# Gate products and the norm's spreading as split fp32r matmuls in place of fp32 ones

## The chip, the cores and the metric

The kernel runs on one core of a Trainium2 chip. The metric is the time of one execution on the device in microseconds (us), the median of a few runs. A core has five engines with a queue each: TensorE (PE in the profile, with its weight loads as PEld), VectorE (DVE), ScalarE (ACT), GpSimd (POOL) and SyncE (SP). Each engine works through its queue in order and waits on semaphores for the others. DMA transfers are issued from the queues of SP and POOL.

## The reference

One layer of a hybrid decoder, for 2048 tokens of width 1024, in float32:

```
h = rms_norm(x, g1)
z = h @ w_in                              # 1024 x 2560: q, k, v, xr, gr, 512 columns each
attn = dilated_attention(q, k, v)         # 8 heads, three dilations, weighted by their denominators
xr = causal_depthwise_conv(xr, conv_w, conv_b)             # 4 taps
r = sigmoid(xr @ w_r + b_r); i = sigmoid(xr @ w_i + b_i)   # in 8 blocks of 64x64
log_a = -8 r softplus(-lam); a = exp(log_a)
u = sqrt(-expm1(2 log_a)) * (i * xr)
rec_t = a_t * rec_(t-1) + u_t             # the recurrence over time
m = concat(attn, rec * gelu(gr)) @ w_out
x = x + rms_norm(m, g2)
h = rms_norm(x, g3)
x = x + rms_norm((relu(h @ w_ff_in) ** 2) @ w_ff_out, g4)
```

## The kernel before

*Products.* An input that a large product needs in more than fp32r's precision is split in two fp32r parts: `split` (lines 54 to 57) casts it into an upper part on ScalarE (line 56) and subtracts this from it for the lower part on VectorE or GpSimd (line 57). A product is then three fp32r matmuls into one bank: upper by upper, upper by lower, lower by upper. `product` does this for the input projection, eight times three matmuls of 128x512 (lines 208 to 210). Two kinds of product in the first part of the kernel are plain fp32 matmuls of unsplit operands: those of the gates and those that spread the norm.

*Stages.* Time is cut in two halves of 1024 tokens, each in two blocks (`b`, or `tb` from 0 to 3) of 512. Until about 600 us the projection of all columns, the recurrence and the attention of the first half are done; then come the output projection and the MLP of the first half, the attention of the second half, and its output projection and MLP. The order of the first part is written out in `ORDER`, `BETWEEN` and `LATER` at the end of the file: "q01" is the q, k and v products of half 0 and head pair 1, "r12" the recurrence of half 1 and channel group 2, "a0" an attention pair, "x2" the loading of block 2. Ahead of this list the groups 0 and 1 of half 0 are done at the start, with weights, x and the norms' inputs loaded from memory at once, into a pool `px` of their own that is given back afterwards.

*The start.* `load_start` loads x of block 0 and the weights of columns 12 and 16 (group 0's xr and gr) in four pieces; their four raw halves lie in tiles "wraw". Weights 13 and 17 (group 1) come through `load_w` with two halves each in the same ring of tiles, of which there are six. All these loads go through `load_next`, which makes each of them be issued on SP's queue behind the one before. `load_norm` (line 137) reads x by rows ("xn") and sums its squares on ScalarE (line 151).

*The norm's spreading.* `spread_norm` turns the factor of each of 512 tokens (tile `r_x`, 128x4) into a 128x512 tile `bc` that has it in every partition: four times a diagonal matrix (`dg`, line 196, VectorE) is multiplied by ones (line 197, TensorE, one fp32 product of 128x128), and the bank is copied out by ScalarE (line 199). It is called four times: for blocks 0 and 1 at the start, for 2 and 3 by "x2" and within "q10".

*A block of the recurrence.* `recurrent_block` runs 16 times (four groups, two halves, two blocks each). The projected xr is scaled out of its bank (line 316, VectorE), the convolution makes `xc` (its first tap on GpSimd, line 319, three on VectorE, line 322), and the two gate products, `pr` (line 325) and `pi` (line 327), multiply `xc` by a 128x128 block-diagonal weight `bd`. ScalarE takes the tanh of both (lines 330 and 332) and then th and the decay r of the sigmoid's output (lines 335 and 336); VectorE makes a2 (line 338), the factor of the input (lines 339, 341, 342) and runs the scan over time (line 343). The gelu of the other columns goes from VectorE (line 347) over GpSimd (lines 350 to 352) back to VectorE (lines 354, 355). The tiles `lt` (th), `la` (a2), `lr` and `li` have one buffer in each pool.

*The order on each engine.* No queue's order stands in the source. `Plan` traces all instructions and lets `Machine` play them through with costs for each kind: each engine takes, of the instructions whose inputs are ready and whose tile is free, the one that is needed first, and TensorE the one that comes first in the program. The resulting order on every engine is then fixed. A change of a few instructions is so planned anew with all others. Each engine takes its instructions in the planned order on the chip, and where a planned input comes later than planned, it waits with all that stand behind.

*Other tiles that the change names.* In the attention of a first half, `fold` (line 420) brings the upper 64 partitions of a bank down, and `join` makes the weights of the two branches in a tile `jt` (lines 691 to 703) that is stored by line 705. `zh` and `zl` hold the parts of q and k on the way to memory, `t512` the scaled products.

Of the kernel before, what the change touches and what calls it, by code (L numbers as in the profile page):

```python
# [9 lines left out]
F32 = mybir.dt.float32  # L10
# [6 lines left out]
P = 128  # L17
# [22 lines left out]
def f32(ap):  # L40
    return ap.bitcast(F32)
# [47 lines left out]
class Project:  # L89
# [14 lines left out]
    def load_w(self, hf, ct, lo_eng=None, px=None):  # L104
# [5 lines left out]
        for half in range(2):  # L110
            k0 = half * (KT // 2)
            raw = (px or self.pa).tile([P, KT // 2, P], F32, tag="wraw", bufs=6 if px else 2, name=f"wraw{hf}_{ct}_{half}")
            self.load_next(raw, self.w_in[ct, :, k0:k0 + KT // 2, :], px)
            split(nc, hi[:, k0:k0 + KT // 2, :], lo[:, k0:k0 + KT // 2, :], raw, lo_eng=lo_eng or self.lo)
        return hi, lo

    def load_start(self, cts, px):
# [4 lines left out]
        raws = {ct: [p.tile([P, KT // 2, P], F32, tag="wraw", bufs=6, name=f"wraw0_{ct}_{i}") for i in range(2)] for ct in cts}  # L122
# [67 lines left out]
    def spread_norm(self, tb):  # L190
# [3 lines left out]
        for j in range(TB // P):  # L194
            dg = self.pa.tile([P, P], F32, tag="dg", bufs=2, name=f"dg{tb}_{j}")
            nc.vector.tensor_scalar(out=dg, in0=self.cst["ident"], scalar1=r[:, j:j + 1], scalar2=None, op0=ALU.mult)
            nc.tensor.matmul(pbc[:, j * P:(j + 1) * P], self.cst["ones"], dg, start=True, stop=True)
# [61 lines left out]
    def recurrent_consts(self, conv_w, conv_b, w_r, b_r, w_i, b_i, lam):  # L259
# [9 lines left out]
        for nm, a in (("r", w_r), ("i", w_i)):  # L269
            t = self.bd[nm] = p.tile([P, 4, P], F32, tag=f"bd_{nm}", name=f"bd_{nm}")  # L270
            g.memset(t, 0.0)
            for u in range(2):
                nc.gpsimd.dma_start(out=t[u * HD:(u + 1) * HD, :, u * HD:(u + 1) * HD], in_=a[u])

# [33 lines left out]
    def recurrent_block(self, hf, c, b, wx, wg, px, zx=None):  # L308
# [15 lines left out]
        pr = self.bank("X", f"pr{n}")  # L324
        pe.matmul(pr, self.bd["r"][:, c, :], xc, start=True, stop=True)
        pi = self.bank("O" if px else "X", f"pi{n}")
        pe.matmul(pi, self.bd["i"][:, c, :], xc, start=True, stop=True)
# [52 lines left out]
def attention(tc, p, bank, cst, scr, hf, mask_a_d, mask_b_d, pj, pw=None, px=None, first=None):  # L380
# [36 lines left out]
    def fold(dst, o, pat, **kw):  # L417

        t = p.tile([HD, TB], F32, tag="fold", bufs=1, name="fold")
# [250 lines left out]
    def join(pr, st, na, nb):  # L670
# [18 lines left out]
        jt = pj.tile([P, TB], F32, tag="jt", bufs=1, name=f"jt{hf}_{pr}")  # L689
# [66 lines left out]
SMB = (3, 4)  # L756
WB = 5
# [1192 lines left out]
def trunk(tc, x, xT, g1, g2, g3, g4, w_in, conv_w, conv_b, w_r, b_r, w_i, b_i, lam, w_out, w1, w2,  # L1950
# [11 lines left out]
    with (  # L1962
# [8 lines left out]
        cst["ones"] = c.tile([P, P], F32, name="ones")  # L1971
        nc.vector.memset(cst["ones"], 1.0)
# [39 lines left out]
        with contextlib.ExitStack() as st:  # L2012
            p1a = st.enter_context(sb("p1a", "left"))
            p1 = st.enter_context(sb("p1", "left"))
# [219 lines left out]
```

## Time and profile before

| | |
|---|---|
| runs | 2175.87 us median of 3 (2174.74 to 2176.11) |
| the profiled execution | 2174.38 us, of which the span of instructions is 2172.6 us |
| TensorE busy | 2136.3 us, 10264 matmul passes |
| VectorE, ScalarE, GpSimd busy | 1520.6, 1229.1, 482.5 us |
| TensorE's clock granted | 0.999 of full speed |
| DMA | 473.51 MB, 218 GB/s in the mean |

Rows of the profile give engine, source line, operation, and output and inputs by their tiles' names, with the number of instructions and their duration. In rows by time the first number is the start in us from the start of the span, the second the length; in brackets stands how long the engine was idle before, and what ended that. Matmuls overlap each other by their latency: the rate is read from the distance of their starts or ends, not from their durations. An fp32 matmul shows as two passes. Rows of windows give the stretch, its length, the busy time of TensorE, its weight loads, VectorE, ScalarE and GpSimd with the number of instructions, then TensorE's clock, the DMA engines' share and the rate in GB/s; where they are asked for one source line, only the engines that this line uses are listed.

### The profile page before, as it was taken

The numbers are of one execution on the slowest core, as the hardware profiler recorded it, in microseconds if no ns is written. First come the engines' busy times: TensorE is split into PE (matmuls) and PEld (weight loads), VectorE is DVE, ScalarE is ACT, GpSimd is POOL, SyncE is SP. The second block draws the span as 40 slices with busy tenths as digits, with TensorE's granted clock in tenths as the row PEclk, the third lists the DMA queues.
The fourth block names the chain that finished last, engine by engine and source line by source line (L and its number), as shares of the span: only waits on it lengthen the run. The fifth ranks groups of instructions, "written<-read, shape, count | busy, mean of one in ns | idle before, by whom it ended". The sixth has DMA issues, their size and how long they took to land.

```text
span 2172.6 us, 30852 instructions
## 1 busy us (share of the span) xinstructions
PE 2136.3 (98%) x10264; PEld 1754.5 (81%) x10264; DVE 1520.6 (70%) x2893; ACT 1229.1 (57%) x2486; POOL 482.5 (22%) x556
## 2 busy tenths in 40 slices
PE   8999999999999999999999999999999999999998
PEld 6777888777788788888888888878788888888887
DVE  7858667858878777775776868787766565664456
ACT  7537566634554655554766667764455555654442
POOL 4652534567523001000010101113100000000003
PEclk9999999999999999999999999999999999999999
DMA  7557686358765667779777785796634444866665
GB/s 249 174 157 212 199 259 194 120 185 296 222 229 180 247 255 296 280 271 356 240 227 222 231 259 170 229 297 192 230 129 174 146 153 146 327 203 193 193 192 183
DMA packets 224548, 473.51 MB, mean 218 GB/s; under 512 B 23476, under 2 KB 79572, under 8 KB 218116
## 3 DMA queue, kind: packets, MB, share of 16 engines
q1 hardware_dynamic: 195572, 337.52, 48.7%
q0 software_dynamic: 28816, 134.01, 17.3%
q8 instruction: 81, 1.33, 0.3%
q14 instruction: 79, 0.65, 0.1%
HBM read 337.09 MB, written 151.13 MB: 225 GB/s over the span
## 4 chain that ended last, share of the span: by engine, by line
PE 84%; DVE 6%; ACT 5%; issue 2%; POOL 2%; DMA 1%; DVEq 0%; POOLq 0%; ACTq 0%; SPq 0%
PE o L1234 9%; PE o L1236 9%; PE o L1235 9%; PE za L1085 5%; PE za L1086 5%; PE za L1084 5%; PE z L210 4%; PE z L209 4%; PE z L208 4%; PE m L871 3%; PE m L870 3%; PE m L869 3%; PE zc L1084 3%; PE zc L1085 3%; PE zc L1086 3%; PE oB L652 2%
## 5 line engine op out<-in xcount | busy, mean ns | idle before, releaser
L208 PE MATMUL z<-hH,wH 128*128 128x512 f32 x640 | 254.6, 399 | 7.3 <-ACT wH L56 5.1
L209 PE MATMUL z<-hL,wH 128*128 128x512 f32 x640 | 256.8, 402 | 0.4 <-DVE hL L183 0.4
L210 PE MATMUL z<-hH,wL 128*128 128x512 f32 x640 | 254.3, 399 | 0.0
L208 PEld LDWEIGHTS z<-hH,wH 128*128 128x128 f32 x640 | 120.7, 189 | 35.0 <-ACT wH L56 5.6
L209 PEld LDWEIGHTS z<-hL,wH 128*128 128x128 f32 x640 | 120.8, 189 | 28.5 <-issue 3.8
L210 PEld LDWEIGHTS z<-hH,wL 128*128 128x128 f32 x640 | 120.8, 189 | 25.7 <-issue 3.6
L57 POOL TENSOR_TENSOR wL<-wraw,wH 128x512 fp32r<-128x512 f32 x70 | 96.0, 1384 | 55.9 <-ACT wH L56 54.4
L1089 ACT ACTIVATE sq<-sq 128x512 f32<-128x512 f32 x93 | 58.8, 632 | 76.6 <-DVE sq L1093 76.6
L1149 POOL DMA_DIRECT2D sa<-sq x31 | 16.5, 532 | 376.6 <-ACT sq L1090 363.7
L432 ACT ACTIVATE smB<-smB,stB 128x128 f32<-128x128 f32 (+3 forms) x128 | 71.5, 560 | 41.5 <-DVE stB L426 41.2
L432 ACT ACTIVATE sm<-sm,stA 128x256 f32<-128x256 f32 (+1 forms) x128 | 63.4, 497 | 53.6 <-DVE stA L426 53.4
L57 DVE TENSOR_TENSOR tlB<-pT_B,thB 128x384 fp32r<-128x384 f32 x96 | 57.1, 598 | 30.4 <-ACT thB L56 27.6
L1090 ACT ACTIVATE sq<-sq 128x512 f32<-128x512 f32 x124 | 76.9, 630 | 2.6
L56 ACT CAST wH<-wraw 128x512 fp32r<-128x512 f32 (+1 forms) x84 | 47.8, 596 | 43.9 <-PE z L209 28.0
L1268 POOL TENSOR_TENSOR y<-y,g4b 128x512 f32<-128x512 f32 x8 | 12.4, 1573 | 257.1 <-ACT junk_y L86 257.1
L426 DVE CUSTOM_DVE_ANT_0 smB<-SB,mask_b 128x128 f32<-128x128 f32 (+3 forms) x128 | 59.3, 485 | 7.3 <-PE SB L627 5.8
L426 DVE CUSTOM_DVE_ANT_0 sm<-S,mask_a 128x256 f32<-128x256 f32 (+1 forms) x128 | 47.5, 408 | 23.4 <-PE S L569 23.3
L405 PE MATMUL pT_B<-ident,smB 128*128 128x128 f32 x320 | 59.9, 277 | 1.7 <-DVE tlB L57 0.9
L240 DVE TENSOR_TENSOR zn<-z,bc 128x512 f32<-128x512 f32 x32 | 22.0, 688 | 54.4 <-PE z L210 52.0
L56 ACT CAST thB<-pT_B 128x384 fp32r<-128x384 f32 x96 | 48.9, 511 | 18.9 <-PE pT_B L405 15.1
L322 DVE SCALAR_TENSOR_TENSOR xc<-xr,cw,xc 128x512 f32<-128x512 f32 x48 | 52.9, 1110 | 6.0 <-POOL xc L319 5.6
L57 POOL TENSOR_TENSOR zl<-zn,zh 128x512 fp32r<-128x512 f32 x28 | 39.4, 1408 | 61.9 <-ACT zh L56 52.5
(607 smaller groups left out, 7075.9 us busy)
## 6 DMA issues: line engine op xcount, KB each, us to landing
sa<-as POOLq DMA_DIRECT2D x31, 1024.0 KB, 6.8
w1r<-in_dram SPq DMA_DIRECT2D x56, 512.0 KB, 4.3
sa<-sq POOLq DMA_DIRECT2D x31, 768.0 KB, 4.0
wraw<-in_dram SPq DMA_DIRECT2D x76, 256.0 KB, 3.5
place<-in_dram SPq DMA_DIRECT2D x14, 1024.0 KB, 6.7
sb<-place POOLq DMA_DIRECT2D x14, 1024.0 KB, 4.2
kh<-sk SPq DMA_DIRECT2D x24, 512.0 KB, 5.1
kl<-sk SPq DMA_DIRECT2D x24, 512.0 KB, 6.8
```

Source lines behind the costliest of these rows:

```text
L57: (lo_eng or nc.vector).tensor_tensor(out=lo, in0=src, in1=f32(hi), op=ALU.subtract))
L208: pe.matmul(z, hi[:, k, :], hh, start=(k == 0), stop=False)
L209: pe.matmul(z, hi[:, k, :], hl, start=False, stop=False)
L210: pe.matmul(z, lo[:, k, :], hh, start=False, stop=(k == KT - 1))
L426: v.tensor_tensor_reduce(out=sm[:, c0:c0 + w], in0=sp[:, c0:c0 + w], in1=mask[:, mask.shape[-1] - w:], scale=1.0, scalar=3.0e38, op0=ALU.a ...
L432: s.activation(out=sm[:, c0:c0 + w], in_=sm[:, c0:c0 + w], func=AF.Exp, scale=-1.0, bias=st[:, 0, u, cols[j]:cols[j] + 1], accum_out=st[:, ...
L1084: pe.matmul(o, hi[:, k], bh[:, k], start=start and k == 0, stop=False, skip_group_check=True)
L1085: pe.matmul(o, hi[:, k], bl[:, k], start=False, stop=False, skip_group_check=True)
L1086: pe.matmul(o, lo[:, k], bh[:, k], start=False, stop=k == KH - 1, skip_group_check=True)
L1234: pe.matmul(o, ah[:, ts], bh, start=fresh and j == 0, stop=False, skip_group_check=True)
L1235: pe.matmul(o, ah[:, ts], bl, start=False, stop=False, skip_group_check=True)
L1236: pe.matmul(o, al[:, ts], bh, start=False, stop=j == NJ - 1, skip_group_check=True)
```

## The change

The gates' products and the norm's spreading become split fp32r products. `xc` is split in parts `xh` and `xl`, in the tiles that th and a2 take later in the same block. The gates' weights are split once, from raw tiles in the ring "t512", into two fp32r tiles each. A gate is then three matmuls of 128x512 into one bank. In the spreading, the factor is split, each part makes four diagonals in one VectorE instruction (in the tiles `zh` and `zl`), and one matmul of 128x512 with ones in fp32r takes each part. To make room, the raw weights of the start have four buffers in place of six, and `jt` of the first half shares the buffer of `fold`, which is taken in full height.

```diff
-            raw = (px or self.pa).tile([P, KT // 2, P], F32, tag="wraw", bufs=6 if px else 2, ...)
+            raw = (px or self.pa).tile([P, KT // 2, P], F32, tag="wraw", bufs=RAWS if px else 2, ...)
...
-        raws = {ct: [p.tile([P, KT // 2, P], F32, tag="wraw", bufs=6, ...
+        raws = {ct: [p.tile([P, KT // 2, P], F32, tag="wraw", bufs=RAWS, ...
...
         pbc = self.bank("X", f"pbc{tb}")
-        for j in range(TB // P):
-            dg = self.pa.tile([P, P], F32, tag="dg", bufs=2, name=f"dg{tb}_{j}")
-            nc.vector.tensor_scalar(out=dg, in0=self.cst["ident"], scalar1=r[:, j:j + 1], scalar2=None, op0=ALU.mult)
-            nc.tensor.matmul(pbc[:, j * P:(j + 1) * P], self.cst["ones"], dg, start=True, stop=True)
+        n = TB // P
+        parts = [p.tile([P, n], F32R, tag=f"rs_{x}", bufs=2, name=f"r{x}{tb}") for x in "hl"]
+        split(nc, *parts, r)
+        for x, part in enumerate(parts):
+            dg = self.pa.tile([P, n, P], F32R, tag=("zh", "zl")[x], bufs=1, name=f"dg{tb}_{x}")
+            nc.vector.tensor_tensor(out=dg, in0=self.cst["ident"].unsqueeze(1).to_broadcast([P, n, P]),
+                                    in1=f32(part).unsqueeze(2).to_broadcast([P, n, P]), op=ALU.mult)
+            nc.tensor.matmul(pbc, self.cst["ones"], dg.rearrange("p n c -> p (n c)"), start=(x == 0), stop=(x == 1))
...
-            t = self.bd[nm] = p.tile([P, 4, P], F32, tag=f"bd_{nm}", name=f"bd_{nm}")
+            t = self.pa.tile([P, 4, P], F32, tag="t512", bufs=3, name=f"bd_{nm}")
+            self.bd[nm] = [p.tile([P, 4, P], F32R, tag=f"bd_{nm}{x}", name=f"bd_{nm}{x}") for x in "HL"]
             g.memset(t, 0.0)
...
+            split(nc, *self.bd[nm], t)
...
-        pr = self.bank("X", f"pr{n}")
-        pe.matmul(pr, self.bd["r"][:, c, :], xc, start=True, stop=True)
-        pi = self.bank("O" if px else "X", f"pi{n}")
-        pe.matmul(pi, self.bd["i"][:, c, :], xc, start=True, stop=True)
+        xh = p.tile([P, TB], F32R, tag="lt", bufs=1, name=f"xh{n}")
+        xl = p.tile([P, TB], F32R, tag="la", bufs=1, name=f"xl{n}")
+        split(nc, xh, xl, xc, lo_eng=GATE_LO and g)
+
+        def gate(tag, nm):
+            z = self.bank(tag, f"p{nm}{n}")
+            hi, lo = [t[:, c, :] for t in self.bd[nm]]
+            pe.matmul(z, hi, xh, start=True, stop=False)
+            pe.matmul(z, hi, xl, start=False, stop=False)
+            pe.matmul(z, lo, xh, start=False, stop=True)
+            return z
+
+        pr = gate("X", "r")
+        pi = gate("O" if px else "X", "i")
...
-        t = p.tile([HD, TB], F32, tag="fold", bufs=1, name="fold")
+        t = p.tile([P, TB], F32, tag="fold", bufs=1, name="fold")[0:HD]
...
-        jt = pj.tile([P, TB], F32, tag="jt", bufs=1, name=f"jt{hf}_{pr}")
+        jt = pj.tile([P, TB], F32, tag="jt" if hf else "fold", bufs=1, name=f"jt{hf}_{pr}")
...
+GATE_LO = None
+RAWS = 4
...
-        cst["ones"] = c.tile([P, P], F32, name="ones")
-        nc.vector.memset(cst["ones"], 1.0)
+        cst["ones"] = c.tile([P, P], F32R, name="ones")
...
+            one = p1a.tile([P, P], F32, tag="zh", bufs=1, name="one")
+            nc.vector.memset(one, 1.0)
+            nc.scalar.copy(out=cst["ones"], in_=one)
```

With `GATE_LO` none, the lower part of `xc` is made on VectorE.

More of the change, by code (lines that the diff above doesn't have):

```diff
@@ L111, in load_w @@
             k0 = half * (KT // 2)
-            raw = (px or self.pa).tile([P, KT // 2, P], F32, tag="wraw", bufs=6 if px else 2, name=f"wraw{hf}_{ct}_{half}")
+            raw = (px or self.pa).tile([P, KT // 2, P], F32, tag="wraw", bufs=RAWS if px else 2, name=f"wraw{hf}_{ct}_{half}")
             self.load_next(raw, self.w_in[ct, :, k0:k0 + KT // 2, :], px)
@@ L121, in load_start @@
             made[ct] = [p.tile([P, KT, P], F32R, tag=f"w{x}", bufs=4, name=f"w{x}0_{ct}") for x in "HL"]
-        raws = {ct: [p.tile([P, KT // 2, P], F32, tag="wraw", bufs=6, name=f"wraw0_{ct}_{i}") for i in range(2)] for ct in cts}
+        raws = {ct: [p.tile([P, KT // 2, P], F32, tag="wraw", bufs=RAWS, name=f"wraw0_{ct}_{i}") for i in range(2)] for ct in cts}
         jobs = list(START)
```

## The prediction

> **What bounds the kernel now.** I read the head of the page first, then the chain, then the windows by stage, then TensorE's own waits, and last the rows of the lines that the diff touches.
>
> ```profile
> span 2172.6 us, 30852 instructions
> PE 2136.3 (98%) x10264; PEld 1754.5 (81%) x10264; DVE 1520.6 (70%) x2893; ACT 1229.1 (57%) x2486; POOL 482.5 (22%) x556
> PEclk9999999999999999999999999999999999999999
> PE 84%; DVE 6%; ACT 5%; issue 2%; POOL 2%; DMA 1%; DVEq 0%; POOLq 0%; ACTq 0%; SPq 0%
> ```
>
> TensorE is busy for 98% of the span at the full clock, and 84% of the chain that ended last lies on it. So work taken off TensorE counts almost one for one, unless the stage in which it lay is one where TensorE waits for something else. Both kinds of stage are there (windows: length, then busy time of each engine):
>
> ```profile
> 0.00:80.00 80.00, 70.88 (x286) 53.06 (x287) 62.36 (x122) 62.95 (x105) 37.83 (x51) 1.00 0.65 222
> 80.00:520.00 440.00, 433.34 (x2289) 353.01 (x2288) 301.92 (x639) 236.62 (x551) 221.47 (x210) 1.00 0.64 197
> 520.00:580.00 60.00, 55.00 (x220) 40.34 (x219) 57.03 (x63) 33.53 (x48) 46.77 (x55) 1.00 0.77 255
> 580.00:2172.00 1592.00, 1577.07 (x7475) 1308.12 (x7473) 1099.29 (x2069) 896.04 (x1785) 176.43 (x243) 1.00 0.67 222
> ```
>
> From 80 to 520 us TensorE is idle for 6.7 of 440 us: its bound. In the first 80 us it is idle for 9.1 us, 5.1 of them before the first weights, and VectorE carries 62.4. From 520 to 580 us VectorE is busy for 57.0 of 60 us and TensorE idle for 5.0: there the recurrence on VectorE sets the pace. TensorE's own waits say the same; the lines of this change are among the first of them (total, times, longest):
>
> ```profile
> PE z L208 <- ACT wH L56: 5.1, 1, 5.1
> PE pr L325 <- DVE xc L322: 4.3, 5, 1.2
> PE pbc L197 <- DVE dg L196: 2.2, 3, 1.3
> PE z L208 <- DVE gr L347: 2.0, 2, 1.7
> ```
>
> **The change, part by part: what TensorE saves.** The chain shows an fp32 gate product as two passes of one product, and the fp32r products after it one by one; the second fence shows how many gate passes there are, and where.
>
> ```profile
> 71.74 0.86 PE pi L327 x2
> ...
> 72.83 0.23 PE z L210
> ...
> 79.90 0.23 PE z L208
> ```
>
> ```profile
> L325 PE MATMUL pr<-xc,bd_r x32: 590/592/697, 38.9 to 573.1; 128*128 128x512 f32 x32
> ...
> 0.00:80.00 80.00, 4.18 (x8) 1.43 (x8) 1.00 0.65 222
> 80.00:520.00 440.00, 8.37 (x16) 2.68 (x16) 1.00 0.64 197
> 520.00:580.00 60.00, 4.47 (x8) 1.19 (x8) 1.00 0.77 255
> ```
>
> An fp32 product takes 0.86 us. From 72.83 to 79.90 there are 31 fp32r steps of the same 128x512 size, so one is 7.07/31 = 0.228 us, and three are 0.68. The 32 passes of L325 are 16 products, those of L327 as many: 32 products, each cheaper by 0.86 - 0.68 = 0.18 us, or **5.7 us**. By stage: 8 products (1.4 us) before 80 us, 16 (2.9) from 80 to 520, 8 (1.4) from 520 to 580. [...]
>
> The norm's spreading, between two fp32r products:
>
> ```profile
> 30.49 0.40 PE L209 MATMUL z<-hL,wH 128*128 128x512 f32 x1
> 30.72 0.61 PE L197 MATMUL pbc<-dg,ones 128*128 128x128 f32 x4
> 31.09 0.47 PE L210 MATMUL z<-hH,wL 128*128 128x512 f32 x1
> 31.40 0.39 PE L208 MATMUL z<-hH,wH 128*128 128x512 f32 x1
> ...
> L197 PE MATMUL pbc<-dg,ones x32: 270/275/377, 28.8 to 328.3; 128*128 128x128 f32 x32
> L196 DVE TENSOR_SCALAR dg<-ident,r_x x16: 272/280/1310, 27.5 to 323.4; 128x128 f32<-128x128 f32 x16
> ```
>
> From 30.49 to 31.40 lie two fp32r steps and four passes of L197: 0.91 - 0.46 = 0.45 us for four, 0.91 for the eight of one spreading. Two fp32r products of 512 columns take 0.46. Four spreadings save 4 x 0.45 = **1.8 us**, half of it at the start. TensorE has 7.5 us less to do in all, 2.3 of them in the first 80 us, 3.8 between 80 and 520, 1.4 between 520 and 580.
>
> **What the other engines get.** Prices from the nearest rows of the same size, and the rows on which the waits rest:
>
> ```profile
> 522.12 0.69 DVE L57 TENSOR_TENSOR e_5L<-e_5L,e_5H 128x512 fp32r<-128x512 f32 x1
> 531.33 3.97 DVE L339 SCALAR_TENSOR_TENSOR th<-a,th 128x512 f32<-128x512 f32 x1
> ...
> 553.78 0.69 DVE L342 TENSOR_TENSOR i<-i,th 128x512 f32<-128x512 f32 x1
> 554.58 1.28 DVE L343 TENSOR_TENSOR_SCAN xc<-r,state,i 128x512 f32<-128x512 f32 x1
> ...
> 23.79 0.60 ACT L56 CAST wH<-wraw 128x512 fp32r<-128x512 f32 x1
> ...
> 555.96 0.69 ACT L330 ACTIVATE r<-pr,vec_br 128x512 f32<-128x512 f32 x1 [0.43 <-DVE xc L343]
> ...
> 572.61 1.12 PE L325 MATMUL pr<-xc,bd_r 128*128 128x512 f32 x2 [1.19 <-DVE xc L322]
> ```
>
> *The split of xc.* Each of the 16 blocks gets an upper part on ScalarE (0.60 us) and a lower part on VectorE (0.69 us), one behind the other, between the last tap of the convolution and the gates. Every block's gates come 1.3 us later, and VectorE has 11 us more in all, ScalarE 10. A gate that still finds its place in TensorE's queue costs nothing; where TensorE already stands at the gate (L325 above, 4.3 us in five waits, 1.19 of it at 572.61) it stands longer. Bounds for one block: 0 and 0.69 + 0.60 + 3.3, the last being what the two-input row at 531.33 took over the 0.69 of an undisturbed one.
>
> From 80 to 520 us I take 0 for the eight blocks: the cover is the products of q, k and v, of 24 steps each, which need nothing from the recurrence. Without that cover it would be 8 x 1.3 = 10 us. From 520 to 580 us the four subtractions are 2.8 us on an engine that is busy 57 of 60; since splits of early factors lie in the same stretch and can give way, I take **2.2 us**. At the start the four blocks come while VectorE is dense, but products of the first queries follow as filler: half of 2.8, **1.4 us**.
>
> *Shared tiles.* The upper part takes th's buffer and the lower part a2's, one each. So the next block's cast waits for L342 of the block before. At 553.78 L342 ends at 554.47; cast, subtraction behind the scan (to 556.5) and the last gate products would put the first tanh near 557.2, where it is at 555.96 now: 1.2 us, the same delay as above and not a second one, as the tanh had to wait for the scan (L343) anyway.
>
> *Raw weights, four buffers for six.* The rows of the start (issue on SP's queue, VectorE, ScalarE, DMA share and rate, TensorE):
>
> ```profile
> 10.95 0.98 SPq L159 DMA_DIRECT2D wraw<-in_dram  x2
> 12.94 2.48 SPq L159 DMA_DIRECT2D xn<-in_dram  x4
> ...
> 15.44 0.76 DVE L57 TENSOR_TENSOR wL<-wraw,wH 128x256 fp32r<-128x256 f32 x2
> ...
> 22.73 1.06 ACT L151 ACTIVATE xn<-xn 128x1024 f32<-128x1024 f32 x1 [0.16 <-DMA xn<-in_dram]
> ...
> 14.00:16.00 2.00, 1.62 (x7) 1.00 (x7) 2.00 (x6) 1.86 (x4) 0.00 (x0) 1.00 1.05 386
> ...
> 28.79 0.71 PE L197 MATMUL pbc<-dg,ones 128*128 128x128 f32 x4 [1.31 <-DVE dg L196]
> ```
>
> The second half of weight 13, issued near 11.4 now, takes the buffer of the second half of weight 12, which is free when the splits at 15.44 are through, near 16. SP's queue issues these loads in a fixed order, so xn, weight 17 and the second block of x all go behind it: about 4.6 us later in the queue. The DMA engines had work queued until some 15 us, so they lose about 2.3 us of a stretch in which they are full (share 1.05). The last xn then comes 2.3 us later than 22.73, and with it the norm, unless ScalarE's order hides some; weight 17 misses its product by about as much. TensorE already stands 1.31 us for that norm at 28.79, and the delay of weight 17 partly takes the place of it. Bounds 0 and 4.6; I take **1.0 us**.
>
> *Small ones.* The spreading's VectorE work goes from 4 x 0.28 to 2 x 0.69 and a small split, 0.5 us more, beside 0.45 less on TensorE before the norm is out: 0, and at most 4 x 0.5 where TensorE waits (L196 above). Its diagonals take the buffers of q's and k's parts, free at the start, and hidden by attention later. The gates' weights are cast at the start, 2 x 0.60 and 2 x 0.69, needed only at 38.9: hidden.
>
> ```profile
> L705 SPq DMA_DIRECT2D sco<-jt x8: 324/335/533, 221.8 to 425.3; - x8
> L691 DVE COPY jt<-pst x4: 269/280/281, 215.2 to 416.6; 16x128 f32<-16x128 f32 x4
> ```
>
> The joining tile now shares its buffer with the folds. It is held from 215.2 to the store at 221.8, 6.6 us, and the next pair's first fold needs it only after a pair's scores: 0, and 6.6 for each of three joins if that cover went.
>
> **Sum.** -7.5 + 1.4 + 2.2 + 1.0 = -2.9 us. The profiled execution took 2174.4 us (span 2172.6), 1.5 below the median of 2175.87; so it becomes 2171.5, and the median **2173.0**, 0.13% faster. No change can be told from one within 0.2%, 4.35 us, with this kernel.
>
> **The rivals.** *The saving comes in full*: the new latency is hidden everywhere, since all queues but TensorE's program order are planned around it and 580 to 600 us has room on VectorE. For it speaks that TensorE's waits for xc are only 4.3 us. 2175.9 - 7.5 = 2168.4.
>
> *All of it is given back*: start and end cost 7 us in place of 4.6, with small losses at the spreadings. 2176 to 2179.
>
> *Slower: VectorE and GpSimd on the shared reads.* The mechanism is the row at 531.33: an operation with two inputs in SBUF that takes 3.97 us in place of 0.69 beside GpSimd's gelu. The change adds 16 such operations, right ahead of the gates. If eight of them (from 455 us and at the start) stand 1.7 us each and TensorE with them, that is 13.6 us against 7.5, 2182; it decides from 1.5 us each. [...] Against it speaks that the undisturbed row of the same subtraction is at 0.69 in the same stretch.
>
> *The change doesn't do what it says*: fp32r products at another rate than 0.228 us. The 31 steps exclude it.
>
> **How the numbers follow.** Forecast, own range 2170 to 2176: 0.42. In full, 2168.4: 0.25. Given back: 0.15. Slower, 2182: 0.18. Faster by over 0.2% (below 2171.5) is the full saving and a third of the forecast's range, 0.39; slower (above 2180.2) 0.18; the rest 0.43. For 8 in 10 I leave out the tails of both outer cases: 2166.5, the full saving with 1.9 us of better order elsewhere (80 to 520 us has 6.7 of idle time), to 2182.
>
> **What would show it.** Right: gate products as three steps of 0.23 us; TensorE's busy time down by about 7; idle time of 520 to 580 us up by some 2; xn issued near 16 us in place of 12.94. Wrong: TensorE's wait for xl growing far past 4.3 us, or the windows after 580 us, in which nothing is edited, moving by more than 2 us.

## The result, and the profile after

The changed kernel takes **2185.72 us** (median of 5, 2181.01 to 2187.01), the kernel before 2175.85 (2174.58 to 2176.11): a ratio of 1.0044 with an interval of [1.0033, 1.0056], 9.9 us slower. The profiled execution took 2181.01 us and is the shortest of the five; the other four have a mean clock of 0.995 or 0.996 in place of its 0.997. So the trace shows 6.6 of the 9.9 us, and the rest lies in the executions with that lower clock, of which there is no trace.

The head of the page of the changed kernel, then its windows by stage (columns as in the prediction):

```profile
span 2179.2 us, 30957 instructions
PE 2138.9 (98%) x10272; PEld 1762.7 (81%) x10272; DVE 1528.1 (70%) x2907; ACT 1244.3 (57%) x2513; POOL 484.3 (22%) x556
```

```profile
0.00:80.00 80.00, 70.77 (x286) 56.19 (x287) 61.88 (x116) 59.61 (x104) 37.74 (x49) 0.98 0.66 225
80.00:520.00 440.00, 433.92 (x2285) 354.85 (x2285) 306.64 (x654) 252.82 (x573) 222.82 (x211) 1.00 0.63 193
520.00:580.00 60.00, 54.31 (x229) 42.18 (x228) 56.89 (x65) 33.22 (x49) 44.86 (x51) 1.00 0.79 264
580.00:620.00 40.00, 36.45 (x156) 28.94 (x155) 27.56 (x41) 19.53 (x32) 7.22 (x8) 0.96 0.77 255
```

TensorE was to be busy for 7 us less and is busy for 2.6 us more. In the last window it is not busy all the time any more, and its clock is below 1.00; the kernel before had this there:

```profile
580.00:620.00 40.00, 40.00 (x182) 33.04 (x181) 23.03 (x39) 20.95 (x36) 6.46 (x8) 1.00 0.83 275
```

**The gates did become three short steps.** TensorE by time, changed kernel, one gate:

```profile
523.41 0.40 PE L337 MATMUL pr<-xh,bd_rH 128*128 128x512 f32 x1
...
524.57 0.39 PE L338 MATMUL pr<-xl,bd_rH 128*128 128x512 f32 x1
524.80 0.39 PE L339 MATMUL pr<-xh,bd_rL 128*128 128x512 f32 x1
525.02 0.40 PE L213 MATMUL z<-hL,wH 128*128 128x512 f32 x1
```

Each takes some 0.23 us, and the order on TensorE has put the cover of two other products between upper and lower part, as foreseen.

**But every step of the input projection has grown.** The product just ahead of this, first in the changed kernel (15 steps), then the same stretch before (18):

```profile
519.68 0.39 PE L214 MATMUL z<-hH,wL 128*128 128x512 f32 x1
...
523.17 0.39 PE L214 MATMUL z<-hH,wL 128*128 128x512 f32 x1
```

```profile
519.71 0.39 PE L210 MATMUL z<-hH,wL 128*128 128x512 f32 x1
...
523.79 0.39 PE L210 MATMUL z<-hH,wL 128*128 128x512 f32 x1
```

3.49/15 = 0.2327 us against 4.08/18 = 0.2267 in these stretches. Over the whole projection the mean step goes from 0.2281 to 0.2313 us (steps between two of its products, without the half clock), and over its 1920 steps that is 6 us.

**And TensorE stands at the start of the output projection.** SP's queue and TensorE by time and a window, all of the changed kernel; then SP's queue before:

```profile
599.33 1.09 SPq L252 DMA_DIRECT2D sk<-zl  x2
601.64 0.38 SPq L260 DMA_DIRECT2D sv<-vs  x1
602.07 3.97 SPq L822 DMA_DIRECT2D woL<-swo  x6
```

```profile
608.07 1.65 PE L887 MATMUL m<-woH,m_0H 128*128 128x512 f32 x3 [2.68 <-ACT woH L56]
```

```profile
602.00:614.00 12.00, 8.54 (x33) 6.48 (x32) 7.92 (x14) 5.98 (x11) 0.60 (x1) 0.86 0.96 343
```

```profile
594.50 5.59 SPq L804 DMA_DIRECT2D woL<-swo  x8
```

The weights of that projection are asked for 7.6 us later. TensorE stands 2.68 us for them, and then the granted clock is at a half, 0.50 from 607.53 to 610.94 us: 0.86 in the mean of the 12 us.

**The account.** Taking the end of each matmul less the end of the one before, against the undisturbed step of its form, TensorE's time up to the first products of the output projection splits into work at undisturbed steps, what the fp32r steps are longer, standing, and what the half clock adds (us, one profiled execution each; start latency and short gaps are in "standing" of both):

| | end | work | longer steps | standing | half clock |
|---|---|---|---|---|---|
| before | 608.9 | 556.5 | 4.2 | 48.3 | 0.0 |
| changed | 615.2 | 548.9 | 10.3 | 53.6 | 2.4 |

Work falls by 7.6 us (the prediction's 7.5), and 6.1, 5.3 and 2.4 come back: 6.2 us later. Up to the last matmul of the kernel the difference is 6.6. Next to nothing more is lost in the 1560 us behind, which were not edited.

### The profile page after: what moved, and what is told of

Read it like the earlier page. It is cut to its first block, busy times and chain, and to the rows that moved or that the text cites. A ratio compares the mean times of both kernels' runs of the same rounds, so it can differ in the third digit from the quotient of the medians.

```text
span 2179.2 us, 30957 instructions
## 1 busy us (share of the span) xinstructions
PE 2138.9 (98%) x10272; PEld 1762.7 (81%) x10272; DVE 1528.1 (70%) x2907; ACT 1244.3 (57%) x2513; POOL 484.3 (22%) x556
## 4 chain that ended last, share of the span: by engine, by line
PE 84%; DVE 5%; ACT 5%; DMA 2%; issue 1%; POOL 1%; SPq 0%; DVEq 0%; ACTq 0%; POOLq 0%
PE o L1252 9%; PE o L1254 9%; PE o L1253 9%; PE za L1103 5%; PE za L1104 5%; PE za L1102 5%; PE z L213 5%; PE z L212 5%; PE z L214 5%; PE m L887 3%; PE m L888 3%; PE m L889 3%; PE zc L1103 2%; PE zc L1102 2%; PE zc L1104 2%; PE oB L668 2%
## 5 line engine op out<-in xcount | busy, mean ns | idle before, releaser
L57 POOL TENSOR_TENSOR wL<-wraw,wH 128x512 fp32r<-128x512 f32 x70 | 96.9, 1395 | 66.2 <-ACT wH L56 65.8
L57 DVE TENSOR_TENSOR tlB<-pT_B,thB 128x384 fp32r<-128x384 f32 x96 | 57.0, 598 | 33.5 <-ACT thB L56 31.1
L244 DVE TENSOR_TENSOR zn<-z,bc 128x512 f32<-128x512 f32 x32 | 22.0, 687 | 48.3 <-PE z L214 47.1
L57 POOL TENSOR_TENSOR zl<-zn,zh 128x512 fp32r<-128x512 f32 x28 | 39.2, 1399 | 69.6 <-ACT zh L56 61.3
L887 PE MATMUL m<-woH,m_0H 128*128 128x512 f32 x128 | 50.7, 404 | 2.7 <-ACT woH L56 2.7
```

What stands on the lines that cost most here:

```text
L57: (lo_eng or nc.vector).tensor_tensor(out=lo, in0=src, in1=f32(hi), op=ALU.subtract))
L887: pe.matmul(o, mh, wh[:, ds], start=(k == order[0]), stop=False)
```

## The experiments

Ratios are to the kernel before, on the same chip. "Aligned" is the changed kernel with the edit of the first experiment. The order of every queue is planned anew wherever instructions change; where the order stayed, it is said.

### Where the tiles lie

The norm's new parts `rs_h` and `rs_l` add 128 bytes per partition ahead of x's lower parts of the second block and the weights. In the kernel before, all tiles of x and of the weights begin at 448 bytes past a multiple of 512; in the changed one, x's upper parts, the first block's lower ones and the weights of the start do, while nearly all of the rest begin at 64. Three kernels with the order of all queues unchanged:

```diff
# e1_after_align, from the changed kernel
-        parts = [p.tile([P, n], F32R, tag=f"rs_{x}", bufs=2, ...
+        parts = [self.pl.tile([P, n], F32R, tag=f"rs_{x}", bufs=2, ...
# e2_before_pad, from the kernel before
-        bcast = p.tile([P, TB], F32, tag="bc", bufs=2, name=f"bc{tb}")
+        bcast = p.tile([P, TB + 16], F32, tag="bc", bufs=2, name=f"bc{tb}")[:, 0:TB]
# e3_after_shift_all, from the changed kernel
-        parts = [p.tile(...
+        parts = [self.pa.tile(...
```

> The changed kernel with one tag moved: the two parts of the norm's factor (128 bytes in a partition) lie in the recurrence's pool in place of the projection's. All instructions and their order on every engine stay the same; only the tiles behind them in the projection's pool move down by 128 bytes, so that x's second block and the weights stand to x's first block at a multiple of 512 bytes, as they did before the change. Theory A, the place in SBUF: the fp32r step of the projection, 231 ns in the changed kernel up to 600 us and 227.5 before, goes back to 227.5; 2000 steps times 3.9 ns, 7 to 8 us less, a time of 2174 to 2179 us. Theory B, the load: the steps are slower because ScalarE and VectorE carry the splits and the order is another one; then the step stays at 231 and the time at 2181 to 2187 us.

> The kernel before with each of the two norm tiles bc taken 64 bytes wider and the rest unused; instructions and orders are those of before, but x's second block and the weights move up by 128 bytes against x's first block. Theory A (place): the step rises from 227.5 to about 231 ns up to 600 us, 7 to 8 us more, 2182 to 2184 us. Theory B (load): no change, 2175 to 2176 us.

> The changed kernel with the parts of the norm's factor in the pool ahead of the projection's: all of x and the weights of after 80 us now have the same remainder by 512 bytes, but another one (64) than before (448); the weights of the start keep 448. Same instructions and orders. If what counts is how the tiles stand to each other: step 227.5 ns from 80 us on, 2175 to 2180 us. If it is the remainder itself: 231 ns, 2181 to 2187 us. Theory B (load): 231 ns, 2181 to 2187 us.

Measured: e1 **2187.46** us (1.0054 [1.0042, 1.0066]), e2 **2179.09** (1.0013 [1.0004, 1.0021]), e3 **2186.49** (1.0050 [1.0039, 1.0061]). The steps do as the placement says. TensorE by time, first the padded kernel before (22 steps), then the aligned changed one (27 steps):

```profile
523.23 0.40 PE L209 MATMUL z<-hL,wH 128*128 128x512 f32 x1
...
528.37 0.40 PE L210 MATMUL z<-hH,wL 128*128 128x512 f32 x1
```

```profile
520.27 0.39 PE L214 MATMUL z<-hH,wL 128*128 128x512 f32 x1
...
526.39 0.39 PE L214 MATMUL z<-hH,wL 128*128 128x512 f32 x1
```

5.14/22 = 0.2336 and 6.12/27 = 0.2267 us. In e3, where x and weights moved together, the mean step is 0.2278 from 80 us on, but 0.2311 before that, where the first weights lie at 448 and x at 64. So in these runs what counts is how the tiles stand to each other; 128 bytes cost 3% of a step in the stretches shown and 1.4% in the mean.

But taking the 6 us away brought nothing. In e1 TensorE arrives earlier at the same waits, stands longer, and the clock falls. Its account: work 548.9, longer steps 4.0, standing 62.1, half clock 10.5, end 625.5. This trace is of the slowest of e1's five executions (2192.41), that of the changed kernel of its fastest, so the two accounts stand further apart than the medians, which are level. This is what makes the rest of the study necessary: in this order the steps got 6 us shorter, and the end did not come earlier. The other way round work does count: in e2's trace, with the order of before, the steps are 6 us longer and the stage ends at 614.6 in place of 608.9, though by the medians the run loses only some 3 us.

### VectorE stands behind GpSimd

The largest new wait of e1 is near 303 us, in the spreading of block 2. VectorE, GpSimd and TensorE of e1 by time, and two windows:

```profile
302.77 4.11 DVE L199 TENSOR_TENSOR dg<-ident,rh 128x512 fp32r<-128x512 f32 x1
306.81 0.28 DVE L442 CUSTOM_DVE_ANT_0 sm<-S,mask_a 128x128 f32<-128x128 f32 x1
...
307.71 0.86 DVE L199 TENSOR_TENSOR dg<-ident,rl 128x512 fp32r<-128x512 f32 x1
```

```profile
302.61 1.29 POOL L57 TENSOR_TENSOR wL<-wraw,wH 128x512 fp32r<-128x512 f32 x1
303.85 1.26 POOL L746 TENSOR_TENSOR na<-na,co 128x512 f32<-128x512 f32 x1
305.07 1.26 POOL L57 TENSOR_TENSOR wL<-wraw,wH 128x512 fp32r<-128x512 f32 x1
306.54 1.48 POOL L749 TENSOR_TENSOR nb<-nb,co 128x512 f32<-128x512 f32 x1 [0.21 <-DMA co<-sco]
```

```profile
307.59 0.55 PE L585 MATMUL S<-kh,qa 128*128 128x256 f32 x1 [3.91 <-DVE stA L442]
```

```profile
303.00:307.00 4.00, 0.67 (x5) 0.40 (x4) 4.00 (x2) 0.00 (x0) 3.79 (x4) 0.83 0.67 164
307.00:313.00 6.00, 5.41 (x22) 4.66 (x23) 3.78 (x16) 4.07 (x15) 3.73 (x4) 0.55 1.05 379
```

The upper diagonals begin 0.16 us after GpSimd's subtraction, and end only when three GpSimd instructions in a row are through and GpSimd pauses (306.33). The softmax's statistics stand behind them, TensorE for these, 3.91 us; then its clock is at 0.55 for 6 us. In the changed kernel as it is, with the same order on every engine, the two operations took 1.11 and 1.73 us:

```profile
302.70 1.11 DVE L199 TENSOR_TENSOR dg<-ident,rh 128x512 fp32r<-128x512 f32 x1
```

```profile
301.95 1.30 POOL L57 TENSOR_TENSOR wL<-wraw,wH 128x512 fp32r<-128x512 f32 x1
303.20 1.74 POOL L746 TENSOR_TENSOR na<-na,co 128x512 f32<-128x512 f32 x1
304.91 1.27 POOL L57 TENSOR_TENSOR wL<-wraw,wH 128x512 fp32r<-128x512 f32 x1
```

GpSimd runs the same three here without a pause. The diagonals arrive 0.75 us after its first one began, end 0.56 us after that one has ended, and GpSimd's second takes 1.74 us in place of 1.26. In e1 they arrived 0.16 us after it and ended 0.55 us after the third. Why it ended behind the first in the one kernel and behind the third in the other isn't shown.

Does the form with one input from SBUF mend it, or a planner that doesn't put these diagonals beside GpSimd?

```diff
# e10_one_input_diagonals, aligned
-            nc.vector.tensor_tensor(out=dg, in0=ident..., in1=f32(part)..., op=ALU.mult)
+            for j in range(n):
+                nc.vector.tensor_scalar(out=dg[:, j, :], in0=self.cst["ident"], scalar1=f32(part)[:, j:j + 1], ...)
# e18_planner_knows_lock, aligned, in Machine.shared
-            big > 1 or big and isinstance(self.ins[k], mybir.InstTensorCopy))
+            big > 1 or big and isinstance(self.ins[k], (mybir.InstTensorCopy, mybir.InstTensorTensor)))
```

> The changed kernel with tiles aligned, and each part's diagonals made as four VectorE operations with one input from SBUF (a scalar per partition) in place of one operation with two. Theory A (the two-input form waits for GpSimd): no diagonal takes over 1.5 us, the 4 us wait of TensorE near 303 us and the half clock behind it are gone; VectorE has 4 x 0.9 us more; time 4 to 6 us below the aligned kernel of before (2187.5), so 2181 to 2184. Rival B (VectorE stands there for another reason, such as a queue order): the wait stays, 2186 to 2189.

> The aligned changed kernel (2187.5), with the planner told that the two-input diagonals cannot run beside GpSimd; the work is the same. If the unknown lock made the wait at 303 us: no diagonal of over 2 us, no wait of TensorE over 2 us between 300 and 310 us, and 3 to 6 us less, 2181 to 2185. If GpSimd's run of instructions there is not foreseen by the planner anyway: the wait stays in some form, and the time is 2185 to 2192.

e10: **2180.32** us (1.0023 [1.0014, 1.0031]), 7 below the aligned kernel. e18: **2181.55** (1.0026 [1.0016, 1.0036]), 6 below. Both times are near those foreseen. In e10 no diagonal takes over 1.88 us and TensorE stands at most 1.9 us for the statistics. But the form isn't what decides. In e18 the first diagonals stand nearly as long as in e1 (3.76 us for 4.11), and TensorE stands 2.0 us, for probabilities in place of statistics; in e16 (below) a small one-input diagonal stands (3.52 us, where the kernel before has 0.28 in the median); and in e14 (below), which spreads the norm in the old way, two subtractions for x do (8.64 us together). VectorE by time of e18, e16 and e14:

```profile
300.24 3.76 DVE L199 TENSOR_TENSOR dg<-ident,rh 128x512 fp32r<-128x512 f32 x1
```

```profile
305.94 3.52 DVE L196 TENSOR_SCALAR dg<-ident,r_x 128x128 f32<-128x128 f32 x1
```

```profile
299.54 8.64 DVE L183 SCALAR_TENSOR_TENSOR hL<-xr,g_sb,hH 128x512 fp32r<-128x512 f32 x2 [1.36 <-ACT hH L182]
```

So the theory that the new two-input form is the cause is too narrow. At this place one of VectorE's SBUF operations stood through a whole run of GpSimd instructions (three in e1, 4.11 us, in e9, 4.10, in e16, 3.52, and in e18, 3.76; five behind the second subtraction of e14), or behind one alone, as in the changed kernel, 1.11 us. The order decides which operation meets GpSimd there; with one and the same order it was 4.11 us in e1 and 1.11 in the changed kernel, which differ in the time of arrival, and what rule this follows isn't shown. That there is a lock, as e18's label and expectation have it, was the author's supposition: the traces show when the operations began and how long they took.

### Each part alone

```diff
# e4_gates_only, from the changed kernel: the spreading's lines as before
-        split(nc, *parts, r)
...
+            nc.vector.tensor_scalar(out=dg, in0=self.cst["ident"], scalar1=r[:, j:j + 1], ...)
# e9_spread_align, from the kernel before: the spreading's lines as changed
+        parts = [self.pl.tile([P, n], F32R, tag=f"rs_{x}", ...
+        split(nc, *parts, r)
...
# e5_before_raws4, from the kernel before (both places)
-            raw = (px or self.pa).tile([P, KT // 2, P], F32, tag="wraw", bufs=6 if px else 2, ...
+            raw = (px or self.pa).tile([P, KT // 2, P], F32, tag="wraw", bufs=4 if px else 2, ...
# e13_share_only, from the kernel before; the order of all queues stays
-        t = p.tile([HD, TB], F32, tag="fold", bufs=1, name="fold")
+        t = p.tile([P, TB], F32, tag="fold", bufs=1, name="fold")[0:HD]
-        jt = pj.tile([P, TB], F32, tag="jt", bufs=1, ...
+        jt = pj.tile([P, TB], F32, tag="jt" if hf else "fold", bufs=1, ...
```

> Only the gates are split, with the four raw buffers and the shared tiles; the norm is spread by fp32 products as before (its diagonals in the two tiles zh and zl in turn), and without the factor's parts the tiles stand as before the change. Theory A: step 227.5 ns; the gates' saving of 5.7 us less what the recurrence's end costs, 2172 to 2179 us. Theory B: 231 ns, 2179 us or more, since nearly all of the added work of ScalarE and VectorE is here. If the output projection stands for its weights near 605 us and the clock falls after it as in the changed kernel, that belongs to the gates' split and not to the spreading.

> The spreading alone as split fp32r products (gates, raw tiles, joining tile as before), with the factor's parts in the recurrence's pool so that x and the weights stand to each other as before. Theory A (the loss is made by the gates' split and by the blocked diagonal, each on its own): the third spreading near 303 us shows a two-input diagonal of about 4 us and TensorE standing 3 to 4 us behind it, the rest is as before; 1.8 us are saved on TensorE, some 4 lost, with half clock after it up to 1.7 more: 2177 to 2181. Rival B (the spreading is harmless and all of the loss is the gates'): 2172 to 2176. Rival C (any newly planned order loses): 2180 or more, with waits in places where nothing is edited.

> The kernel before with four raw tiles at the start in place of six; nothing else is edited, and the orders differ only in the first 80 us. If the ring is a cost of the change: xn issued near 16 us in place of 12.94, TensorE idle 1 to 4.6 us more in the first 100 us, 2176 to 2181 us. If the start hides it: within 1 us of the kernel before.

> The kernel before with only the joining tile sharing the buffer of the folds; the order of every queue stays as before. If the shared buffer makes the waits of TensorE for the joins near 325 us seen in the changed kernel, they appear here too and the time rises by 2 to 6 us: 2178 to 2182. If it doesn't: 2175 to 2177, no wait of over 1 us there.

Measured: gates alone **2183.97** (1.0040 [1.0027, 1.0053]); spreading alone **2189.69** (1.0066 [1.0054, 1.0079]); four raw buffers 2175.18 (0.9994 [0.9985, 1.0003]); shared joining tile 2176.89 (1.0004 [0.9995, 1.0013]). The last two cost nothing. The smaller edit costs the most: spreading alone is slower than both together. In e9 the diagonals of 303 us stand again (4.10 us, from 305.0), with further waits where nothing is edited (2.60 us for xc from 562, 2.98 for zn from 585) and five stretches of half clock before the output projection (7.1 us in its account below). Its trace, too, is of the slowest of its executions. Losses that are not additive, and do not grow with the edit, point to the order.

### The gates' work and their wait

```diff
# e7_no_xl, aligned
-        split(nc, xh, xl, xc, lo_eng=GATE_LO and g)
+        s.copy(out=xh, in_=xc)
-            pe.matmul(z, hi, xl, start=False, stop=False)
# e8_lo_pool, aligned: the lower part of xc on GpSimd
-GATE_LO = None
+GATE_LO = True
# e14_split_unused, from the kernel before: no product reads xh or xl
+        xh = p.tile([P, TB], F32R, tag="lt", bufs=1, name=f"xh{n}")
+        xl = p.tile([P, TB], F32R, tag="la", bufs=1, name=f"xl{n}")
+        split(nc, xh, xl, xc)
         pr = self.bank("X", f"pr{n}")
         pe.matmul(pr, self.bd["r"][:, c, :], xc, start=True, stop=True)
```

> The changed kernel with the tiles back in place, without the lower part of xc: each gate is upper by upper and lower by upper, which leaves out the product with xl, and VectorE's subtraction with it. 32 products (7.3 us) and 16 subtractions (11 us of VectorE) less. If VectorE and its place in the chain between convolution and gates set the first 600 us: waits for the gates fall by more than a half, and the time falls by more than the 7.3 us of the products, to 2172 to 2178 us. If TensorE's work sets it: 7 us less than 2187, 2180. If it is neither (the order, the other engines): the idle time grows by what the products save, 2185 to 2188 us.

> The changed kernel with the tiles back in place, and the lower part of xc subtracted by GpSimd in place of VectorE: 1.3 us for 0.69 in each of 16 blocks. If VectorE's load costs the time: VectorE has 11 us less, 2 to 6 us less than 2187. If the latency between convolution and gates does: 0.6 us more for each block, 2187 to 2193 us, with longer waits for the gates' second product.

> The kernel before with xc split in its two parts in all 16 blocks (in the tiles of th and a2, as in the change), but the gates stay fp32 products of the whole xc and wait for neither part; the parts are not read by any product. Theory A1 (the added work on VectorE and ScalarE, with the shared tiles, makes the loss of the gates): 2180 to 2185. Theory A2 (the gates' longer way from xc to the product makes it): 2175 to 2179.

Measured: e7 **2181.33** (1.0024 [1.0013, 1.0035]), e8 **2185.07** (1.0038 [1.0026, 1.0051]), e14 **2179.09** (1.0015 [1.0006, 1.0024]). e7 leaves out one of a gate's three terms and is 6 us below the aligned kernel, for 7.3 us less of work and 16 subtractions less; that is no more than a new order of the aligned kernel brings by itself (e12 below). Against the kernel before it has 541.6 us of work for 556.5, 14.9 less, and is still slower: standing is 62.7 for 48.3 and the half clock takes 5.6. Of those 14.9 us nothing reaches the end. Its time is nearest to the one foreseen if TensorE's work sets the pace (2180), but as a new order alone brings as much, e7 can't tell the two apart; what speaks against it is that the shorter steps of e1 and e3 brought nothing in an order that stayed. The lower part on GpSimd changes little. The unused split costs 3 us, at the upper end of what was foreseen if the gates' longer way made the loss, and under what was foreseen if the added work made it. The largest new wait in its trace is the one behind the 8.64 us above (TensorE 5.0 us for the statistics), not one at a gate.

### The loads of the output projection

```diff
# e6_wo_pool, aligned
-            nc.sync.dma_start(out=f32(lo[:, ds]), in_=w_out[k][:, ds])
+            (nc.sync if hf else nc.gpsimd).dma_start(...)
```

> The changed kernel with the tiles back in place, and the first half's output weights loaded from GpSimd's queue in place of SP's; the orders differ from the run with the tiles in place only around 600 us. Theory C: these loads stand in SP's queue behind the stores of the last k and v, come late, TensorE stands 3.3 us for woH and the clock falls after it; then both go, 4 to 7 us less than the 2187 us with the tiles in place alone, 2180 to 2183 us. Rival: the loads wait for memory that the recurrence gives back, not for the queue; then the wait for woH stays, and the time within 2 us of 2187.

**2192.93** us (1.0075 [1.0063, 1.0088]), slower still. GpSimd's queue and TensorE's waits from 600 us:

```profile
607.19 0.60 POOL L373 DMA_DIRECT2D smix<-ge  x1 [8.77 <-DVE ge L371]
607.79 3.68 POOL L822 DMA_DIRECT2D woL<-swo  x7
```

```profile
PE m L887 <- ACT woH L56: 4.8, 1, 4.8
```

Gates alone, e9, e10 and e12 have no wait for woH at all, and e12 does the same work as e1, which has 2.74 us of it: this wait, too, comes with the order. On SP's queue the loads stood behind stores of q and k; here they stand behind the last store of the recurrence, which waits 8.77 us for a VectorE operation planned behind another product. A better queue wasn't found; whether the loads could go earlier on any queue stays open.

### The order

One constant of the planner (the time from an engine's end to TensorE's start) was changed, which alters no instruction and replans every queue:

```diff
-SLACK = 0.8
+SLACK = 0.9   # e11_before_new_plan, the kernel before
+SLACK = 0.7   # e17_before_plan_07, the kernel before
+SLACK = 0.7   # e12_aligned_new_plan; e15_one_input_new_plan; e16_gates_new_plan (gates alone)
```

> The kernel before with one constant of its planner changed (the time between an engine's end and TensorE's start taken as 0.9 us in place of 0.8), so that every queue's order is planned anew while the work is the same. Theory C (before's order is a lucky one, and any new plan loses 5 to 10 us): 2180 or more. Theory A (the loss belongs to the added work): within 3 us of before, 2173 to 2179.

> The aligned changed kernel with the same constant of the planner at 0.7 in place of 0.8: the same work in another order. Theory C (the order was an unlucky one): 2180 or less is possible, as much above or below the aligned kernel's 2187.5 as the before kernel moves with its new plan. Theory A (the loss belongs to the added work): 2184 to 2191, the waits near 80, 303 and 530 us being there again.

> The aligned changed kernel with one-input diagonals and the planner's constant at 0.7 in place of 0.8. If the two gains (7 us by the diagonals, 6 by the other order) add: 2172 to 2177, level with before or below it. If the other order only happened to avoid the same wait: 2178 to 2183.

> The gates alone (spreading as before) with the planner's constant at 0.7. If the 8 us of the gates alone were the order: 2173 to 2178. If they belong to the split and the wait for it: 2181 to 2187, with idle time of TensorE again at 80, 320 and 540 to 580 us.

> The kernel before with the planner's constant at 0.7 in place of 0.8, the same value with which the gates alone went to 2195.9 and the one-input version to 2190.2. If the large moves come with this value of the constant: 2185 or more here too. If they come with the changed work, whose waits leave TensorE idle long enough for the half clock: 2174 to 2180, with under 2 us of half clock before 600 us.

| same work, us | constant 0.8 | another |
|---|---|---|
| before | 2175.85 | 2177.16 (0.9), 2183.67 (0.7) |
| changed, aligned | 2187.46 | 2181.32 (0.7); 2181.55 (e18) |
| the same with one-input diagonals | 2180.32 | 2190.20 (0.7) |
| gates alone | 2183.97 | 2195.88 (0.7) |

e17 has the ratio 1.0038 [1.0025, 1.0050], e11 1.0007 [0.9998, 1.0015], e12 1.0031 [1.0020, 1.0043], e15 1.0074 [1.0061, 1.0088], e16 1.0098 [1.0084, 1.0112]. With not one instruction changed, the kernel before becomes 7.8 us slower, most of what the change cost. TensorE's waits of e17 from 520 to 600 us, and the windows around the longest:

```profile
PE pr L325 <- DVE xc L322: 4.9, 4, 2.8
```

```profile
552.00:556.00 4.00, 1.39 (x4) 0.84 (x5) 3.98 (x6) 0.89 (x2) 3.44 (x5) 0.96 1.06 400
556.00:560.00 4.00, 4.00 (x13) 3.16 (x12) 3.59 (x5) 2.35 (x3) 0.00 (x0) 0.61 1.06 320
```

The same signature: TensorE stands 2.8 us for VectorE, and the granted clock of the 4 us behind is 0.61. The time lies between the two expectations, nearer to the one that blames the constant's value; but 0.7 made the aligned kernel faster, so the value isn't bad in itself. It is the order that it happens to give. e15 and e16 lie above both of the ranges foreseen for them, so neither gains that add nor a loss that is the split's own explains them.

The account to the output projection for these, in the columns from above: e9 554.5, 3.7, 60.4, 7.1; e10 548.9, 4.1, 54.6, 4.2; e12 548.9, 4.2, 58.9, 4.1; e17 556.2, 4.1, 52.7, 3.1. All have more standing and more half clock than before (48.3 and 0.0), and the end follows these two, not the work.

**What is shown and what isn't.** Shown: TensorE's work falls as computed; the placement adds 6 us of steps; what comes back besides is standing, for VectorE and ScalarE and for loads, and half clock behind long waits (a mean clock of 0.86, 0.55 and 0.61 in the windows shown); another order of the same work moves the time by up to 12 us. Not settled: how much of the 9.9 us belongs to the change. Over the orders tried the kernel before has a mean of 2178.9 (three), the aligned changed one 2183.4 (three): 4.5 us, with a spread of 6 to 8 us inside each, which doesn't separate them. No version with the change or a part of its products was faster than the kernel before, and none that beats it was found.

## Why the prediction was wrong, point by point

*What TensorE saves*: right, 7.5 predicted, 7.6 in the account, gates in three steps of 0.23 us.

*"So work taken off TensorE counts almost one for one"*: this is the step that failed. It was read from a busy share of 98% and from 6.7 us of idle time between 80 and 520 us. Busy time there is not the same as being the bound: the matmul records overlap, so the windows show 20.8 us of idle time up to 600 us where the account finds 48.3 of standing up to 608.9. In one and the same order, steps made 6 us shorter brought nothing (e1 and e3 against the changed kernel), and e7, with 14.9 us less of work than the kernel before, was slower than it. The sum kept all waits as they were except those at edited places; in the trace the saving went into 5.3 us of standing and 2.4 of half clock, the longest new wait being 2.68 us for the output projection's weights.

*The sum had no term for the place of the tiles*: 128 new bytes lengthened 1920 steps, 6.1 us in the profiled execution. It stood in the diff, as two tiles of 4 columns by two buffers, and was taken for nothing. On the kernel before it costs some 3 us (1.0013); in the changed one its removal gives nothing; in e1's trace what it frees goes into standing and half clock.

*The spreading's VectorE work at 0, at most 4 x 0.5*: the bound was too small. In the changed kernel's own trace the diagonals near 303 us took 1.11 and 1.73 us, and TensorE's wait behind them was 1.0 us at most; in the aligned kernel one of them took 4.11 us, with 3.9 us of standing and a clock of 0.55 in the 6 us behind.

*The splits from 80 to 520 us at 0, with a cover by q, k and v*: the cover held on TensorE (the order puts two products between the gate's parts). What was left out is the other side: the unused split, for whose parts no gate waits, costs 3 us in its own order.

*Start, 1.4 and 1.0 us*: xn is issued at 14.42 us in place of 12.94, in the direction foreseen and a third of the 4.6 us; the raw ring alone costs nothing (0.9994). The joining tile, 0 taken: right (1.0004).

*520 to 580 us, 2.2 us*: TensorE's busy time there is 54.31 against 55.00, less than foreseen. A part of the loss lies just behind, at the handover to the output projection, which the prediction named only as a sign ("the windows after 580 us"): TensorE is busy for 3.5 us less there.

*The rival "slower", 2182*: its time is the nearest to what was measured, by luck for the most part. Its place was wrong: of the 16 subtractions of xc none took over 1.76 us. VectorE beside GpSimd does cost several us at another place, but in other runs: TensorE's longest wait near 303 us is 3.91 us in e1, 3.9 in e9, 5.0 in e14, 3.1 in e16 and 2.0 in e18, and 1.0 at most in the changed kernel's own trace. The row at 531.33 that it rests on stood beside GpSimd's weight subtractions (L57, from 531.45 and 533.47) and the first tap of a convolution (L319, from 532.73), not beside the gelu; that the two engines share their reads, as its name has it, no run shows. It was weighed at 0.18 because the same operation was found undisturbed once; the right reading would have been that one operation can take very different times beside GpSimd (1.11 and 4.11 us with the same order, in the changed kernel and in e1), so that a new order draws anew at all such places. And no rival priced the half clock, of which the trace of before has one stretch of 3.41 us, from 1576.38, and the last 2.3 us of the span.

## What to carry to other kernels

Where all queues are planned anew, an edit of a few microseconds is below what the order itself moves, here up to 12 us: replan the unchanged kernel a few times first, and count as gain only what exceeds that spread. A busy engine isn't the bound if shortening its work only lengthens its waits; test it by shortening its work while every queue keeps its order. When tiles are added, compare the offsets of the large operands before and after.

## What the hardware showed that was not expected

- In these runs the rate of a 128x512 fp32r product went with how its operands stand to each other in SBUF: 0.2267 us with all at the same remainder by 512 bytes (the kernel before and e1), 0.2327 and 0.2336 with some 128 bytes off (the changed kernel and e2) in the stretches shown; 0.2281 and 0.2313 in the mean of the projection, in the kernel before and in the changed one. Why isn't known.
- In the traces of before and of the changed kernel the granted clock is at full or at a half, and from 9.66 and 10.20 us on, where its record begins, each stretch is a whole number of steps of 3.413 us, but for the last, which ends with the span: 459, 1 and 173 steps in before, 1, 1, 173, 1, 285, 1 and 173 in the changed kernel. Of these, 1264 are at full clock. All six in which TensorE's matmul records leave 2.13 us or more idle, the last of each trace among them, were followed by half clock, and none of the 1258 with 1.60 us or less. So in these traces the idle time within one step tells the two apart, and the length of a wait does not: in before a wait of 1.74 us (from 558.52) fell 0.69 and 1.04 us into two steps and left the clock at full, while one of 1.70 us (from 1572.94) and the first 1.00 us of the next one (from 1575.38) left 2.68 us of one step idle, and the half clock followed; in the changed kernel the stand of 2.68 us (from 605.39) and a short one ahead of it left 2.76 us of one step idle, and the half clock followed. What lies between 1.60 and 2.13 us isn't shown.
- A VectorE operation that met a run of GpSimd instructions ended behind one of them or behind several: after 1.11 us in the changed kernel, behind the first of three without a pause, after 4.11 us in e1, behind the third of the same three; two subtractions of e14 took 8.64 us together, the second of them ending behind five. VectorE had arrived 0.16 us after GpSimd in e1 and e9 (4.11 and 4.10 us), 0.30 in e16 (3.52), 0.57 in e18 (3.76) and 0.75 in the changed kernel (1.11); what decides isn't known.
